# Spare products, late modulation and scan loads moved in a one-core f32 MLA + DeltaNet + ConvGLU layer

## The chip, the cores and the metric

One core of one Trainium2 chip runs the whole layer in one launch. The metric is the device time of one execution in microseconds (us); lower is better. A run of a kernel is timed several times, and a separate execution is recorded by the hardware profiler. PE is the matmul engine (TensorE), DVE the vector engine (VectorE), ACT the scalar engine (ScalarE), POOL is GpSimd, and SP (SyncE) issues most of the DMA transfers. Each engine carries out its own list of instructions in order, and waits where an operand or a buffer isn't ready.

## The reference, cut to what matters

One layer over 256 latent tokens `x` and 256 context tokens `ctx`, width 2048, all in f32. Only the latent stream is put out.

```
sh1,sc1,g1,sh2,sc2,g2 = split(silu(c) @ w_ada + b_ada)        # modulation, 6 x 2048
p      = modulate(rmsnorm(x), sh1, sc1) @ w_in                # columns split into:
         q_a, kv_a, k_r (attention), dq, dk, dv, dz, da, db (DeltaNet), two gates
y_mla  = attention of 8 heads: q from rmsnorm(q_a) @ w_q_b, k and v from
         rmsnorm(kv_a) @ w_kv_b, rms norm over q and k, rotary part, softmax over
         256 latent and 256 context keys
y_dn   = gated DeltaNet of 8 heads in chunks of 64, one scan forward, one backward,
         started from the final states of the context
y      = (sigmoid(gate_mla) * (y_mla @ w_o_mla) + sigmoid(gate_dn) * (y_dn @ w_o_dn)) @ w_out
x      = x + g1 * y
x      = x + g2 * (silu(dwconv(h @ w_gate)) * (h @ w_val)) @ w_down,
         h = modulate(rmsnorm(x), sh2, sc2)
```

## The kernel before, in words

**Products.** Every weight comes in as f32. `load_w` brings it into a ring of eight raw buffers of 128x1024 (tag `raw`), and splits each half of 512 columns: ACT casts the high part `whi` (L122), DVE subtracts it from the raw weight and so makes the low part `wlo` (L123). `split` does the same for activations. `mm_hl` multiplies a tile of 128x128: `whi` with the high and low parts of the activation side by side (128x512), then `wlo` with the high part (128x256). These two are called a pair here. `row_bcast` spreads a column vector over all partitions by f32 products with the identity.

**Stages.** Modulation and first projections (names `amp`, `fp`) to about 141 us of the profiled span; the first heads' projections (`mmp`) with the decay masks of the DeltaNet (`cps`, `gp`, `eps`), to about 195; the other heads' DeltaNet chains, to about 430; the latent attention (`kps`, `vps`, `qps`, `sps`, `yps`), to about 720; the DeltaNet scan over eight steps (`yp`, `kp`, `sp_`, `op`), to about 901; the products of the two branches (`brp`); the output product (`ops`), 948 to 1041; the norm before the FFN; the FFN's up products (`fps`) to 1527, and its down products (`dps`).

**Late modulation.** The part of the modulation that is needed late is 128 tiles of 128x1024 f32 (`rawa`, in the same ring as the weights). `ada_rest` loads two ahead, and one multiply-reduce on DVE (L268 within the scan and the stages behind it, an operation that the order lists as ISA) sums a tile against `sch`, a row that is read back from memory (`Sc`). Column blocks 0 to 2 must be done before the norm of the FFN.

**Order.** `Side` is a generator with a budget: a call adds nanoseconds, and the generator goes on as long as it has budget; a tile of late modulation costs 1300. Budgets: `ADB` in the DeltaNet chains, `AD` in the attention, `ADS` in the scan, `WO` per output tile, 1000 per FFN tile. `fill` is another such generator: it brings the products of gate tiles (`gtp`, 16 pairs each, yielding after each four) between the attention's and the scan's steps. With `pe.pinned` true, PE's products stand in the order in which the code issues them; otherwise, and on the other engines, the compiler's scheduler chooses. SP's DMAs go in the order of issue; in the compiled program each also waits for the landing of the DMA eight before it.

**The scan.** `scan()` allocates its memory at the place that the attention's last products (`yps`) free. For a step it loads V, the triangular system (`tt`, six small loads from `Xq` and `Xo`) and the keys `KEs`, and KTs, all into `jit` and `tt`. The first step has no state yet, so that its KTs aren't used. `warm(n)` issues n spare products with the identity that compute nothing, two records each.

Of the kernel before, what the change touches and what calls it, by code (L numbers as in the profile page):

```python
# [42 lines left out]
OC = 4000  # L43
WO = 1500
IK = 7000
# [3 lines left out]
R1 = 0.9  # L49
ADB = 4000  # L50
SCALE = 192.0 ** -0.5


@with_exitstack
def hybrid_block(ctx: ExitStack, tc: tile.TileContext, io, dbg=None):
# [88 lines left out]
    def lazy_w(src):  # L144

        cur = [None, None]

        def W(o, m=P):
            if cur[0] != o // GR:
                cur[:] = o // GR, load_w(src[:, o // GR * GR : min(o // GR * GR + GR, src.shape[1])])  # L150
            return cur[1](o % GR, m)

        return W

# [32 lines left out]
    class Rms:  # L187
# [17 lines left out]

        def finish(self, mul, out):
            n, pl = self.n, self.pl
            ms = pl.tile([P, 4], F32, tag="ms", name="ms", bufs=1)[:, :n]
            dve.tensor_scalar(out=ms, in0=self.ss[:, :n], scalar1=mul, scalar2=EPS, op0=ALU.mult, op1=ALU.add)
            rsq(pl, ms, ms, n)  # L210
            bc_ps = psa.tile([P, 512], F32, tag="aux", name="bc_ps")
            row_bcast(bc_ps, ms, n)
            if out is not None:
                act.copy(out.rearrange("p a b -> p (a b)"), bc_ps[:, : n * P])
            return bc_ps

    def rms_bcast(pl, K, src, mul, out):
        r = Rms(pl, K, len(src(0)))
        for k in range(K):
            r.add(*src(k))  # L220
        return r.finish(mul, out)

# [236 lines left out]
    mod_cols(0, False, *later)  # L459
    warm(9)  # L460
    H = [hp.tile([P, KD, 2, T], F32R, tag="h", name="h0"), ph.tile([P, KD, 2, T], F32R, tag="h", name="h1")]
# [316 lines left out]
    ada.done, ada.bound = 0, True  # L778
    ins = {h: head_inputs(h) for h in (3, 0)}

# [115 lines left out]

    def gate_tiles(jobs):

        for w, f, out, fin in jobs:
            W = lazy_w(io[w][f])  # L900
            ps = psm.tile([P, 512], F32, tag="mm", name="gtp")
            for k in range(KD):
                mm_hl(ps, P, W(k * P), H[0][:, k], k == 0, k == KD - 1)
                if k == 3 and late:
                    late.pop()()
                if k % 4 == 3 and k < KD - 1:
                    yield 1300
            gate_fin(ps, out, fin)
            yield 1300
# [21 lines left out]
    bq = pn.tile([P, 1, T], F32, name="bq")  # L931
    rms_bcast(pn2, 4, lambda k: (qax[:, k],), 1.0 / 512, bq)
    for k in range(4):
# [31 lines left out]
    fill(5200)  # L965
    bk = rms_bcast(pn2, 4, lambda k: (kvx[:, k, 0], kvx[:, k, 1]), 1.0 / 512, None).rearrange("p (a b) -> p a b", a=2)
    fill(9000)
# [10 lines left out]
    def mm3(ps, a, b, first, last):  # L978

        pe.matmul(ps, a[0], b[0], start=first, stop=False)  # L980
        pe.matmul(ps, a[0], b[1], start=False, stop=False)
        pe.matmul(ps, a[1], b[0], start=False, stop=last)

    def mla_project(b):
# [58 lines left out]
        v_tile(1)  # L1043
        yield 3500
        v_tile(2)
        v_tile(3)
# [4 lines left out]
        k_scale(km0, 0)  # L1051
        for j in range(2):
            q_tile(j)
        k_scale(km1, 1)
        yield 3500
# [124 lines left out]
    fill.finish()  # L1180
    gates = gate_tiles([("wgd", f, f - GD0, None) for f in range(GD0, KD)])
    pC.close()
# [34 lines left out]
    def scan():  # L1217
        pS = ExitStack()
        ps1 = pS.enter_context(pool_("scan", 1, "right"))
        jit = ps1.tile([P, 6, 1024], F32, name="jit")  # L1220
        TTv = [ps1.tile([P, HEADS, 64], F32, name=f"tt{n}") for n in range(2)]
        av = ps1.tile([P, HEADS, 64], F32, name="av")
        for n in range(2):
            pool.memset(TTv[n], 0.0)
        half_ = [slice(0, 64), slice(64, 128)]
        S = ps1.tile([P, HEADS, 2, P], F32, name="S")
        steps = (4, 5, 6, 7, 0, 1, 2, 3)

        def load_kv(n):
            kt, v = (jit[:, 2 * j + n % 2].rearrange("p (h c) -> p h c", c=P) for j in (0, 2))  # L1230
            sync.dma_start(kt, KTs[steps[n]])
            sync.dma_start(v, Vs[steps[n]])
            return kt, v
# [10 lines left out]
        def load_ke(n):  # L1244
            ke = jit[:, 2 + n % 2].rearrange("p (h c) -> p h c", c=P)
            sync.dma_start(ke, KEs[steps[n]])
            return ke
# [10 lines left out]
        for n, st in enumerate(steps):  # L1258
# [23 lines left out]
            if last:  # L1282
                zo = jit[:, 2:4].rearrange("p a (h t) -> p (a h) t", t=T)
                sync.dma_start(zo, Zs)
# [365 lines left out]
```

## Time and profile before

| | |
|---|---|
| time, median of 3 runs | 1770.11 us (1768.79 to 1772.45) |
| the profiled execution | 1771.28 us |
| its span | 1769.5 us |
| PE busy | 1743.7 us, 99% |
| DVE busy | 1324.0 us, 75% |
| ACT busy | 939.4 us, 53% |
| mean granted clock of PE | 0.996 |
| moved by DMA | 415.08 MB, 235 GB/s on the mean |

The profile is one execution recorded by the hardware. A row of a timeline starts with its start in us and the time that it lasts; then engine, line of the kernel, operation, output<-inputs, the shape, how many instructions it holds, and in brackets the idle time of the engine before it with what ended it. A row of a group has the number of instructions, then busy us in all and mean ns of one, then the idle time before them and what ended most of it. In a row of waits stand the us waited in all, how often, and the longest. Windows give busy us of PE, PEld (PE's weight loads), DVE, ACT and POOL in a stretch, the granted clock of PE (1.00 is full speed), the busy share of the DMA engines and GB/s.

### The profile page before, as it was taken

Reading aid. Unit: us, or ns where it says so; the run is one execution under the profiler, and the core shown is the slowest. Engines: PE = TensorE matmul, PEld = TensorE weight load, DVE = VectorE, ACT = ScalarE, POOL = GpSimd, SP = SyncE. Lnnn points to the kernel's source line nnn. Section 1 sums busy time; section 2 is a strip of 40 time slices with the busy share of each in tenths; the row PEclk is TensorE's granted clock in tenths of the full one; section 3 lists DMA queues with packets and bytes.
Section 4 is the critical chain, followed back from the end, with each engine's and each line's share of the span. In section 5 each row is a group of like instructions: output and inputs, shape, how many; then the busy total and the mean of one; then the engine's idle time right before and its main releaser. Section 6 shows DMA issues by size and latency. Waiting matters only on the chain.

```text
span 1769.5 us, 34499 instructions
## 1 busy us (share of the span) xinstructions
PE 1743.7 (99%) x13173; PEld 1517.7 (86%) x13173; DVE 1324.0 (75%) x2576; ACT 939.4 (53%) x1953; POOL 48.6 (3%) x49
## 2 busy tenths in 40 slices
PE   8999999999999999999999999999999999999999
PEld 6788888888888988887888898888888888888888
DVE  4687788769777878586789789888778888755554
ACT  3335544444666666555656455555555555544443
POOL 0000011000000000000010000000000000000000
PEclk9999999999999999999999999999999999999999
DMA  9992588783677867997967858777666777666662
GB/s 382 392 365 93 167 233 245 228 257 117 215 245 249 263 206 261 296 328 244 332 192 239 290 175 288 228 224 236 215 191 225 225 226 226 207 199 199 199 196 86
DMA packets 188710, 415.08 MB, mean 235 GB/s; under 512 B 56768, under 2 KB 95040, under 8 KB 186240
## 3 DMA queue, kind: packets, MB, share of 16 engines
q1 hardware_dynamic: 162944, 397.92, 69.0%
q10 hardware_dynamic: 25600, 14.96, 2.7%
q8 instruction: 103, 1.69, 0.4%
q14 instruction: 63, 0.52, 0.1%
HBM read 386.21 MB, written 26.48 MB: 233 GB/s over the span
## 4 chain that ended last, share of the span: by engine, by line
PE 89%; DMA 6%; DVE 3%; issue 1%; ACT 1%; POOL 0%; SPq 0%; DVEq 0%; ACTq 0%; POOLq 0%
PE fps L69 27%; PE dps L69 14%; PE mmp L69 13%; PE gtp L69 9%; PE ops L69 5%; PE brp L69 4%; PE fp L69 4%; PE vps L69 1%; DMA raw<-in_wadab 1%; PE kps L69 1%; PE amp L69 1%; DVE wlo L123 1%; PE sps L69 1%; PE tp L69 1%; DMA raw<-in_wgd 1%
## 5 line engine op out<-in xcount | busy, mean ns | idle before, releaser
L123 DVE TENSOR_TENSOR wlo<-raw,whi 128x512 fp32r<-128x512 f32 (+1 forms) x940 | 634.9, 685 | 228.9 <-ACT whi L122 218.9
L122 ACT CAST whi<-raw 128x512 fp32r<-128x512 f32 (+1 forms) x940 | 572.9, 619 | 377.6 <-PE dps L69 113.7
L69 PE MATMUL fps<-H,whi 128*128 128x512 f32 x1376 | 472.4, 392 | 0.0
L69 PE MATMUL fps<-H,wlo 128*128 128x256 f32 x1376 | 371.4, 280 | 0.0
L69 PEld LDWEIGHTS fps<-H,whi 128*128 128x128 f32 x1376 | 252.5, 188 | 50.7 <-DVE fx L509 0.2
L69 PEld LDWEIGHTS fps<-H,wlo 128*128 128x128 f32 x1376 | 258.4, 188 | 7.4 <-DVE wlo L123 0.5
L69 PE MATMUL gtp<-h,whi 128*128 128x512 f32 x640 | 230.5, 398 | 0.2
L69 PE MATMUL mmp<-h,whi 128*128 128x512 f32 x640 | 226.8, 397 | 0.0
L69 PE MATMUL dps<-GB,whi 128*128 128x512 f32 (+1 forms) x595 | 195.7, 378 | 0.0
L69 PE MATMUL gtp<-h,wlo 128*128 128x256 f32 x640 | 173.4, 281 | 2.6 <-DVE wlo L123 2.5
L69 PE MATMUL mmp<-h,wlo 128*128 128x256 f32 x640 | 175.8, 281 | 0.0
L69 PE MATMUL dps<-GB,wlo 128*128 128x256 f32 x560 | 154.1, 280 | 0.0
L69 PEld LDWEIGHTS gtp<-h,whi 128*128 128x128 f32 x640 | 119.3, 188 | 25.3 <-ACT whi L122 1.2
L69 PEld LDWEIGHTS mmp<-h,whi 128*128 128x128 f32 x640 | 119.0, 188 | 24.7 <-issue 0.4
L69 PEld LDWEIGHTS gtp<-h,wlo 128*128 128x128 f32 x640 | 120.5, 188 | 8.4 <-DVE wlo L123 4.2
L69 PEld LDWEIGHTS dps<-GB,whi 128*128 128x128 f32 x595 | 109.2, 188 | 21.2
L69 PEld LDWEIGHTS mmp<-h,wlo 128*128 128x128 f32 x640 | 120.3, 188 | 2.7 <-issue 0.6
L268 DVE CUSTOM_DVE_ANT_0 rawa<-rawa,sch 128x1024 f32<-128x1024 f32 x71 | 86.6, 1221 | 29.3 <-DMA rawa<-in_wada 29.1
L69 PEld LDWEIGHTS dps<-GB,wlo 128*128 128x128 f32 x560 | 105.1, 188 | 0.6
L69 PE MATMUL fp<-h,gh 128*128 128x256 f32 (+1 forms) x448 | 84.3, 289 | 0.7 <-DVE h L69 0.7
L69 PEld LDWEIGHTS fp<-h,gh 128*128 128x128 f32 (+1 forms) x448 | 68.8, 188 | 6.1 <-issue 4.5
L69 DVE CUSTOM_DVE_ANT_0 rawa<-rawa,sch 128x1024 f32<-128x1024 f32 x57 | 69.1, 1217 | 0.0
(564 smaller groups left out, 2553.2 us busy)
## 6 DMA issues: line engine op xcount, KB each, us to landing
rawa<-in_wada SPq DMA_DIRECT2D x128, 512.0 KB, 4.6
raw<-in_wgate SPq DMA_DIRECT2D x82, 512.0 KB, 4.4
raw<-in_wval SPq DMA_DIRECT2D x82, 512.0 KB, 5.0
raw<-in_wdown SPq DMA_DIRECT2D x80, 512.0 KB, 4.3
wt<-in_wadas SPq DMA_DIRECT2D x16, 1024.0 KB, 10.2
raw<-in_wadab SPq DMA_DIRECT2D x32, 512.0 KB, 11.9
raw<-in_wgm SPq DMA_DIRECT2D x32, 512.0 KB, 4.6
raw<-in_wgd SPq DMA_DIRECT2D x32, 512.0 KB, 6.2
```

The lines of the kernel that those rows point to most:

```text
L69: i = f(*a, **k)
L122: act.copy(hi, raw)
L123: dve.tensor_tensor(out=lo, in0=raw, in1=hi, op=ALU.subtract)
L268: (odve if ada.bound else dve).tensor_tensor_reduce(out=w, in0=w, in1=sch, scale=1.0, scalar=0.0, op0=ALU.mult, op1=ALU.add, accum_out=par ...
```

## The change

Eight edits:

1. `WO` is 1100 in place of 1500: a smaller budget of late modulation per output tile.
2. `ADE` = 0.35: the projections of the first two heads call late modulation between their products, which they did not.
3. `warm` blocks shrink: 9 to 7 in the modulation, 7 and 7 to 3 and 4, and 14 to 7 at the norm of the FFN.
4. `finish` of the norm calls a side: between the reciprocal root on POOL and the broadcast, four pairs of a gate tile are issued, in both norms of the attention's ranks.
5. `k_scale` (8 calls) broadcasts a vector in another way: DVE spreads it on diagonals (`diag`, a high and a low part), and two f32r products of 128x512 with a matrix of ones replace four f32 products of 128x128. DVE's part is issued one or two `v_tile`s ahead.
6. In the last attention block late modulation is left out from the second step on, not from the fifth on.
7. `gate_tiles` in the scan asks for its weights a portion ahead: `need(1)` at k = 4, the next branch's weights at k = 12, and a branch asks for the next gate tile's first portion at k = 3.
8. The scan's memory is laid out anew, so that what the first step loads (`jit0`, `tt0`) lies in memory that is free before the attention ends. The first step's KTs is not loaded.

```diff
-WO = 1500
+WO = 1100
+ADE = 0.35
...
     def lazy_w(src):
-        cur = [None, None]
+        got = {}
+        def need(i):
+            if i not in got:
+                got[i] = load_w(src[:, i * GR : min(i * GR + GR, src.shape[1])])
         def W(o, m=P):
-            if cur[0] != o // GR:
-                cur[:] = o // GR, load_w(src[:, o // GR * GR : min(o // GR * GR + GR, src.shape[1])])
-            return cur[1](o % GR, m)
+            need(o // GR)
+            return got[o // GR](o % GR, m)
+        W.need = need
         return W
...
             rsq(pl, ms, ms, n)
+            side(1300)
             bc_ps = psa.tile([P, 512], F32, tag="aux", name="bc_ps")
...
-    warm(9)
+    warm(7)
...
-    ins = {h: head_inputs(h) for h in (3, 0)}
+    ins = {h: head_inputs(h, lambda c: ada(c * ADE)) for h in (3, 0)}
...
+            W = Ws[j] if Ws else lazy_w(io[w][f])
             for k in range(KD):
+                if Ws and k == 4:
+                    W.need(1)
+                if Ws and k == 12:
+                    after(j)
...
+    def diag(r):
+        rh = pc2.tile([P, 4], F32R, tag="rb_h", name="rb_h")
+        rl = pc2.tile([P, 4], F32, tag="rb_l", name="rb_l")
+        dve.tensor_copy(rh, r)
+        dve.tensor_tensor(out=rl, in0=r, in1=rh, op=ALU.subtract)
+        idb = ident.unsqueeze(1).broadcast_to([P, 4, P])
+        dg = []
+        for v in (rh, rl):
+            d = pc2.tile([P, 4, P], F32R, tag="rb_d", name="rb_d")
+            dve.tensor_tensor(out=d, in0=idb, in1=v.unsqueeze(2).broadcast_to([P, 4, P]), op=ALU.mult)
+            dg.append(d)
+        return dg
...
         def k_scale(km, h2):
+            dg = diag(km)
+            yield 500
             bp = psa.tile([P, 512], F32, tag="aux", name="kbp")
-            row_bcast(bp, km, 4)
+            for n in range(2):
+                pe.matmul(bp, onesr, dg[n].rearrange("p a b -> p (a b)"), start=n == 0, stop=n == 1)
...
-                    side(c, R1 if b < 3 else 2.0, b == 3 and n > 3)
+                    side(c, R1 if b < 3 else 2.0, b == 3 and n > 0)
...
+    bW, gW = {}, [lazy_w(io["wgd"][f]) for f in range(GD0, KD)]
+    gates = gate_tiles([("wgd", f, f - GD0, None) for f in range(GD0, KD)], gW, branch_next)
...
-        W = load_w(io[w][f])
+        W = load_w(io[w][f]) if wh else bW.pop(f)
...
             if k == 3:
                 yield 1300
+                if not wh:
+                    gate_next(f + 1)
...
-        jit = ps1.tile([P, 6, 1024], F32, name="jit")
-        TTv = [ps1.tile([P, HEADS, 64], F32, name=f"tt{n}") for n in range(2)]
+        jit = ps1.tile([P, 4, 1024], F32, name="jit")
+        TTv = [None, ps1.tile([P, HEADS, 64], F32, name="tt1")]
...
+        jit0 = ps1.tile([P, 2, 1024], F32, name="jit0")
+        TTv[0] = ps1.tile([P, HEADS, 64], F32, name="tt0")
...
-            sync.dma_start(kt, KTs[steps[n]])
+            if n:
+                sync.dma_start(kt, KTs[steps[n]])
             sync.dma_start(v, Vs[steps[n]])
...
-        warm(7)
+        warm(3 + rms.k - 1)
...
-    warm(14)
+    warm(7)
```

Where instructions moved, at three places. First SP's list around the first loads of the scan; `raw` are weights, `rawa` late modulation, `jit` and `tt` the scan's operands. Before:

```order
L249 DMA rawa<-in_wada 128x1024
L128 DMA raw<-in_womla 128x1024
L128 DMA raw<-in_wgd 128x1024 x2
L128 DMA raw<-in_womla 128x1024
L249 DMA rawa<-in_wada 128x1024 x2
L128 DMA raw<-in_wgd 128x1024
L249 DMA rawa<-in_wada 128x1024
L1231 DMA jit<-KTs 128x1024
L1232 DMA jit<-Vs 128x1024
L1241 DMA tt_8700<-Xq 32x8x32 x2
L1241 DMA tt_8700<-Xo 32x8x32
```

and of the changed kernel, at the same place of SP's list:

```order
L129 DMA raw<-in_womla 128x1024
L255 DMA rawa<-in_wada 128x1024
L129 DMA raw<-in_wgd 128x1024 x2
L255 DMA rawa<-in_wada 128x1024
L129 DMA raw<-in_womla 128x1024
L1284 DMA jit_8778<-Vs 128x1024
L1293 DMA tt_8779<-Xq 32x8x32 x2
L1293 DMA tt_8779<-Xo 32x8x32
L1293 DMA tt_8779<-Xq 32x8x32 x2
L1293 DMA tt_8779<-Xo 32x8x32
L1298 DMA jit_8778<-KEs 128x1024
```

The load of KTs is gone, and weights of the second branch product stand ahead of V and the system in the place of late modulation.

Second, DVE's list in the first heads, where the decay gate `gx` is worked out (`plx` is a polynomial of it, `ghl` its high and low parts, `B` the masks built from it). Before:

```order
L570 TENSOR_SCALAR plx<-w2x 128x64
L123 TENSOR_TENSOR wlo<-raw,whi 128x512
L572 SCALAR_TENSOR_TENSOR plx<-plx,w2x 128x64 x6
L573 SCALAR_TENSOR_TENSOR plx<-plx,zx 128x64
L575 SCALAR_TENSOR_TENSOR xg<-plx,xg 128x64
L579 SCALAR_TENSOR_TENSOR gx<-xg,ea 128x64
```

and of the changed kernel:

```order
L578 SCALAR_TENSOR_TENSOR plx<-plx,w2x 128x64
L70 ISA rawa,parts<-rawa,sch 128x1024
L70 ISA parts 128x1
L578 SCALAR_TENSOR_TENSOR plx<-plx,w2x 128x64
L124 TENSOR_TENSOR wlo<-raw,whi 128x512
L578 SCALAR_TENSOR_TENSOR plx<-plx,w2x 128x64 x2
L579 SCALAR_TENSOR_TENSOR plx<-plx,zx 128x64
L124 TENSOR_TENSOR wlo<-raw,whi 128x512
L581 SCALAR_TENSOR_TENSOR xg<-plx,xg 128x64
L585 SCALAR_TENSOR_TENSOR gx<-xg,ea 128x64
```

The first three rows stand there three times one after the other, and a fourth tile of late modulation stands some rows above; before, none of the 128 stood ahead of `gx`.

Third, DVE's list in a step of the scan (`r` is the new value's right side, `gk` a finished gate, `ox` and `t` the branch product's end). Before:

```order
L509 TENSOR_TENSOR gk<-gtp,gk 128x256
L268 ISA rawa,parts<-rawa,sch 128x1024
L268 ISA parts 128x1
L1210 SCALAR_TENSOR_TENSOR ox<-brp,ox 128x256
L1211 SCALAR_TENSOR_TENSOR t_8685<-gt,ox 128x256
L1276 SCALAR_TENSOR_TENSOR r<-kp,negc,jit 128x128 x8
L123 TENSOR_TENSOR wlo<-raw,whi 128x512 x4
```

and of the changed kernel, around the eight `r` of such a step:

```order
L515 TENSOR_TENSOR gk<-gtp,gk 128x256
L124 TENSOR_TENSOR wlo<-raw,whi 128x512
L274 ISA rawa,parts<-rawa,sch 128x1024
L274 ISA parts 128x1
L1256 SCALAR_TENSOR_TENSOR ox<-brp,ox 128x256
L1257 SCALAR_TENSOR_TENSOR t_8754<-gt,ox 128x256
L1328 SCALAR_TENSOR_TENSOR r<-kp,negc,jit_8778 128x128 x8
L124 TENSOR_TENSOR wlo<-raw,whi 128x512 x2
```

Before, four low parts stood behind the eight `r`; in the changed kernel two stand behind it, and the others ahead of it.

More of the change, by code (lines that the diff above doesn't have):

```diff
@@ L204, in add_sq, with finish @@
             self.k += 1
-        def finish(self, mul, out):
+        def finish(self, mul, out, side=lambda c: None):
             n, pl = self.n, self.pl
@@ L215, in finish, with rms_bcast @@
             return bc_ps
-    def rms_bcast(pl, K, src, mul, out):
+    def rms_bcast(pl, K, src, mul, out, side):
         r = Rms(pl, K, len(src(0)))
@@ L220, in rms_bcast @@
             r.add(*src(k))
-        return r.finish(mul, out)
+        return r.finish(mul, out, side)
     class Side:
@@ L895, in gate_fin, with gate_tiles @@
                 late.pop()()
-    def gate_tiles(jobs):
-        for w, f, out, fin in jobs:
-            W = lazy_w(io[w][f])
+    def gate_tiles(jobs, Ws=None, after=None):
+        for j, (w, f, out, fin) in enumerate(jobs):
+            W = Ws[j] if Ws else lazy_w(io[w][f])
             ps = psm.tile([P, 512], F32, tag="mm", name="gtp")
             for k in range(KD):
+                if Ws and k == 4:
+                    W.need(1)
+                if Ws and k == 12:
+                    after(j)
                 mm_hl(ps, P, W(k * P), H[0][:, k], k == 0, k == KD - 1)
@@ L931, in hybrid_block @@
     bq = pn.tile([P, 1, T], F32, name="bq")
-    rms_bcast(pn2, 4, lambda k: (qax[:, k],), 1.0 / 512, bq)
+    rms_bcast(pn2, 4, lambda k: (qax[:, k],), 1.0 / 512, bq, fill)
     for k in range(4):
@@ L965, in hybrid_block @@
     fill(5200)
-    bk = rms_bcast(pn2, 4, lambda k: (kvx[:, k, 0], kvx[:, k, 1]), 1.0 / 512, None).rearrange("p (a b) -> p a b", a=2)
+    bk = rms_bcast(pn2, 4, lambda k: (kvx[:, k, 0], kvx[:, k, 1]), 1.0 / 512, None, fill).rearrange("p (a b) -> p a b", a=2)
     fill(9000)
@@ L1044, in mla_project @@
         yield 3500
+        sc0, sc1 = k_scale(km0, 0), k_scale(km1, 1)
+        next(sc0)
         v_tile(2)
+        next(sc1)
         v_tile(3)
@@ L1050, in mla_project @@
         qsq = pc2.tile([P, 3, T], F32, tag="qsq", name="qsq", bufs=1)
-        k_scale(km0, 0)
+        for _ in sc0:
+            pass
         for j in range(2):
             q_tile(j)
-        k_scale(km1, 1)
+        for _ in sc1:
+            pass
         yield 3500
@@ L1180, in hybrid_block, with branch_next, gate_next @@
     fill.finish()
-    gates = gate_tiles([("wgd", f, f - GD0, None) for f in range(GD0, KD)])
+    bW, gW = {}, [lazy_w(io["wgd"][f]) for f in range(GD0, KD)]
+    def branch_next(f):
+        if f < KD:
+            bW[f] = load_w(io["womla"][f])
+    def gate_next(f):
+        if f < len(gW):
+            gW[f].need(0)
+        else:
+            branch_next(f)
+    gates = gate_tiles([("wgd", f, f - GD0, None) for f in range(GD0, KD)], gW, branch_next)
     pC.close()
@@ L1219, in scan @@
         ps1 = pS.enter_context(pool_("scan", 1, "right"))
-        jit = ps1.tile([P, 6, 1024], F32, name="jit")
-        TTv = [ps1.tile([P, HEADS, 64], F32, name=f"tt{n}") for n in range(2)]
+        jit = ps1.tile([P, 4, 1024], F32, name="jit")
+        TTv = [None, ps1.tile([P, HEADS, 64], F32, name="tt1")]
         av = ps1.tile([P, HEADS, 64], F32, name="av")
+        half_ = [slice(0, 64), slice(64, 128)]
+        S = ps1.tile([P, HEADS, 2, P], F32, name="S")
+        for tag, shape, bufs in (("r", [P, 4, P], 2), ("y", [P, 2, 4, P], 1), ("qe", [P, HEADS, P], 1), ("osq", [P, 4, 2, 64], 2)):
+            for _ in range(bufs):
+                ps1.tile(shape, F32, tag=tag, name=tag, bufs=bufs)
+        jit0 = ps1.tile([P, 2, 1024], F32, name="jit0")
+        TTv[0] = ps1.tile([P, HEADS, 64], F32, name="tt0")
         for n in range(2):
             pool.memset(TTv[n], 0.0)
-        half_ = [slice(0, 64), slice(64, 128)]
-        S = ps1.tile([P, HEADS, 2, P], F32, name="S")
         steps = (4, 5, 6, 7, 0, 1, 2, 3)
         def load_kv(n):
-            kt, v = (jit[:, 2 * j + n % 2].rearrange("p (h c) -> p h c", c=P) for j in (0, 2))
-            sync.dma_start(kt, KTs[steps[n]])
+            kt, v = (x.rearrange("p (h c) -> p h c", c=P) for x in ((jit[:, 2], jit[:, 3]) if n % 2 else (jit[:, 0], jit0[:, 0])))
+            if n:
+                sync.dma_start(kt, KTs[steps[n]])
             sync.dma_start(v, Vs[steps[n]])
@@ L1244, in load_ke @@
         def load_ke(n):
-            ke = jit[:, 2 + n % 2].rearrange("p (h c) -> p h c", c=P)
+            ke = (jit[:, 1] if n % 2 else jit0[:, 1]).rearrange("p (h c) -> p h c", c=P)
             sync.dma_start(ke, KEs[steps[n]])
@@ L1282, in scan @@
             if last:
-                zo = jit[:, 2:4].rearrange("p a (h t) -> p (a h) t", t=T)
+                zo = jit[:, 0:2].rearrange("p a (h t) -> p (a h) t", t=T)
                 sync.dma_start(zo, Zs)
```

## The prediction

> **What bounds the kernel now.** I read the head of the page first (busy shares, then the chain that ended last).
>
> ```profile
> span 1769.5 us, 34499 instructions
> PE 1743.7 (99%) x13173; PEld 1517.7 (86%) x13173; DVE 1324.0 (75%) x2576; ACT 939.4 (53%) x1953; POOL 48.6 (3%) x49
> PE 89%; DMA 6%; DVE 3%; issue 1%; ACT 1%; POOL 0%; SPq 0%; DVEq 0%; ACTq 0%; POOLq 0%
> ```
>
> PE is busy for 1743.7 of 1769.5 us, so PE's products are the time: the kernel gets shorter only where products disappear, where one of PE's 26 us of gaps closes, or where PE runs at a higher granted clock. Work added on DVE or DMA is free as long as PE does not wait for it. So I took each edit to its place on PE's timeline and asked which wait, or which product, goes there. The profiled execution took 1771.28 us (1.78 around the span) against the median of 1770.11; the sum is made against 1771.28.
>
> **A. Spare products at the seam before the FFN.** The timeline of PE, ACT, DVE and POOL there, and PE's group of spares (two records for a spare):
>
> ```profile
> L69 PE MATMUL warm<-ident 128*128 128x128 f32 x80 | 10.2, 280 | 0.0
> 1041.47 1.83 PE L69 MATMUL warm<-ident 128*128 128x128 f32 x14
> 1041.86 0.42 ACT L1456 ACTIVATE x1q<-x 128x256 f32<-128x256 f32 x1
> 1043.23 0.31 PE L69 MATMUL ss<-ones,x1q 128*32 128x1 f32 x16
> 1043.47 1.83 PE L69 MATMUL warm<-ident 128*128 128x128 f32 x14
> 1043.84 0.70 POOL L174 TENSOR_TENSOR ms<-ms,half 128x2 f32<-128x2 f32 x1 [145.11 <-DVE ms L1471]
> 1045.13 0.61 PE L69 MATMUL b<-ident,ms 128*128 128x128 f32 x4
> 1045.58 3.29 PE L69 MATMUL warm<-ident 128*128 128x128 f32 x28
> 1046.84 0.88 DVE L1485 SCALAR_TENSOR_TENSOR H<-h,adaT,H 128x256 fp32r<-128x256 f32 x2 [0.19 <-ACT H L1484]
> ```
>
> One spare takes 3.29 / 14 = 0.235 us (10.2 / 40 = 0.26 over all). First block, 7 to 3: its operand x1q is ready at 1041.86 + 0.42 = 1042.28, the product started at 1043.23; three spares end at about 1042.25, so 0.95 us go. Second, 7 to 4: POOL's ms ends 1044.54, the product b started 1045.13; POOL's work hangs on the sum in front of it and moves along with it, and four spares cover all but 0.1 of it, so 0.5 go. Third, 14 to 7: 7 x 0.235 = 1.6, they would end at 1047.2, and the FFN's first low part H on DVE (two tiles in the row) is done at 1046.84 + 0.44 = 1047.28, so PE would hardly wait; but the other tiles of H come in DVE's pace, and I let 0.7 of the 1.6 be lost to it. The two spares taken from the modulation stage stand before a wait of PE anyway and give 0. **A: -2.3** (0 to -3.4).
>
> **B. Row broadcast of the k norm** (8 calls): four f32 products of 128 columns become two f32r products of 512.
>
> ```profile
> L69 PE MATMUL kbp<-ident,km 128*128 128x128 f32 x64 | 8.6, 277 | 0.0
> L69 PE MATMUL sps<-kt,qt 128*128 128x512 f32 x48 | 14.6, 413 | 0.0
> L69 PE MATMUL gp<-B,onesr 64*128 64x512 f32 x16 | 4.2, 468 | 0.0
> L123 DVE TENSOR_TENSOR wlo<-raw,whi 128x512 fp32r<-128x512 f32 (+1 forms) x940 | 634.9, 685 | 228.9 <-ACT whi L122 218.9
> 560.00:580.00 20.00, 20.00 (x178) 17.52 (x177) 13.41 (x30) 12.90 (x31) 3.29 (x2) 1.00 0.71 212
> ```
>
> Before, a call costs 8.6 / 8 = 1.07 us of PE. The same two products are not in the trace; the neighbours are 128x512 products of the attention, 14.6 / 48 = 0.30, and of the masks against onesr, 4.2 / 16 = 0.26. Two of them: 0.52 to 0.61, so 8 calls save 3.7 to 4.4. I take -4.1. DVE gets per call two multiplies of 128x512 (0.69 each by wlo) and two tiny ones, about 1.7 us, 14 us in all. What hides it: DVE is busy 13.41 of 20 us in the MLA stage (the window above; its columns after the length are PE, PEld, DVE and ACT), and the multiplies are issued one or two v tiles ahead of the products. Where a weight's low part queues behind them, PE waits; two-sided, 0 to +2, I take +1. **B: -3.1** (-4.4 to -1.7).
>
> **C. Gate products during the reciprocal root.** PE's group for the broadcast of a rank norm:
>
> ```profile
> L69 PE MATMUL bc_ps<-ident,ms 128*128 128x128 f32 x20 | 3.0, 290 | 2.0 <-POOL ms L174 2.0
> ```
>
> PE idles 2.0 us in front of these for POOL. Of its calls two get four pairs of a gate tile (eight such products ahead of each), 1.4 us or more of work that was due anyway, which covers 0.9 each. **C: -1.5** (0 if that tile's low weight parts come late, -2.0 at most).
>
> **D. First step of the scan.** Timelines of PE, SP and DVE, and the windows of 20 us (last columns: granted clock, DMA share, GB/s):
>
> ```profile
> 704.61 1.23 DVE L268 CUSTOM_DVE_ANT_0 rawa<-rawa,sch 128x1024 f32<-128x1024 f32 x1 [1.23 <-DMA rawa<-in_wada]
> 706.83 1.67 PE L69 MATMUL yps<-PT,V 128*128 128x512 f32 x8 [1.64 <-DVE PT L123]
> 716.23 0.30 SPq L1241 DMA_DIRECT2D tt<-Xo  x1
> 719.19 2.52 PE L69 MATMUL yp<-jit,tt 64*64 64x128 f32 x32 [2.36 <-DMA tt<-Xo]
> 722.23 0.41 PE L69 MATMUL brp<-YM,wlo 128*128 128x256 f32 x1
> 722.87 0.41 PE L69 MATMUL brp<-YM,wlo 128*128 128x256 f32 x1
> 700.00:720.00 20.00, 16.00 (x95) 13.47 (x97) 14.84 (x28) 10.75 (x24) 0.53 (x1) 0.98 0.66 190
> 720.00:740.00 20.00, 20.00 (x163) 17.17 (x159) 6.32 (x16) 10.51 (x27) 0.00 (x0) 0.85 0.99 302
> ```
>
> The window of 700 to 720 holds PE's largest gap: 4 of 20 us. Two waits make it. yps waited 1.64 because DVE's PT stood behind a late-modulation tile that itself waited for its DMA; the change takes late modulation out of that block, so some 1.4 go. Then yp waited 2.36 for the last tt load, issued only at 716.23, eight DMAs after the load of jit (which had to wait for memory of the attention). With step 0 loading into memory that is free already, the queue has no such wait at its head: the tt loads can all be issued some 5 us earlier, and 2.36 goes. Third, after that gap the clock is down: 0.85 over 720 to 740 is (1 - 0.85) x 20 = 3.0 us lost, and a pair of products takes 722.87 - 722.23 = 0.64 there. No gap, no drop: 3.2. The gate products brought forward by C (2.8 us for two calls) are missing here, so PE arrives at yp 2.8 us and the vanished waits earlier; that is why I do not call it safe. **D: -7.0** (-1.4, if only the first wait goes, to -8.0).
>
> The trace has the lower clock right behind an idle time of 2.36 us, and none behind the idle times of 1.64 here or 1.55 and 1.82 below. The Trainium skill (TensorE: Matmul & The Clock Gate, section "What's actually happening") has the half rate come only after an idle window of about 3.4 us. By that figure alone the drop would not belong to this gap, the clock would not return with it, and the sum would end 3.2 us higher; here the trace disagrees with it, and the trace decides.
>
> **E. Gate weights of the scan a portion ahead.** Waits of the engines between 686 and 902 us, and the longest of these on DVE and PE:
>
> ```profile
> PEld gtp L69 <- DVE wlo L123: 4.2, 5, 1.9
> PE gtp L69 <- DVE wlo L123: 2.5, 4, 1.6
> PEld gtp L69 <- ACT whi L122: 1.2, 4, 0.5
> 801.78 2.16 DVE L1276 SCALAR_TENSOR_TENSOR r<-kp,negc,jit 128x128 f32<-128x128 f32 x8 [2.52 <-PE kp L69]
> 803.86 2.48 DVE L123 TENSOR_TENSOR wlo<-raw,whi 128x512 fp32r<-128x512 f32 x4
> 804.60 0.39 PE L69 MATMUL gtp<-h,wlo 128*128 128x256 f32 x1 [1.55 <-DVE wlo L123]
> ```
>
> A low part asked for only when its product is due queues behind the scan's r on DVE (2.52 of wait and 2.16 of work), and PE stops. A portion ahead, two low parts stand before r in DVE's order. I take 3.0 of the 4.2 + 1.2. **E: -3.0** (0 to -5.4).
>
> **F. Fewer late-modulation tiles in the output product.** DVE there, and PE's group:
>
> ```profile
> L69 PE MATMUL ops<-MB,wlo 128*128 128x256 f32 x128 | 33.8, 283 | 2.8 <-DVE wlo L123 2.8
> 1001.15 1.23 DVE L268 CUSTOM_DVE_ANT_0 rawa<-rawa,sch 128x1024 f32<-128x1024 f32 x1 [2.69 <-DMA rawa<-in_wada]
> 1003.38 0.39 PE L69 MATMUL ops<-MB,wlo 128*128 128x256 f32 x1 [1.82 <-DVE wlo L123]
> ```
>
> All 2.8 us stand behind a tile that waits for its DMA in DVE's queue. Ten of them stand between the first and the last output tile in place of fourteen: **F: -1.8** (0 to -2.8).
>
> **G. What it costs: the first heads.**
>
> ```profile
> L268 DVE CUSTOM_DVE_ANT_0 rawa<-rawa,sch 128x1024 f32<-128x1024 f32 x71 | 86.6, 1221 | 29.3 <-DMA rawa<-in_wada 29.1
> 149.52 1.52 DVE L572 SCALAR_TENSOR_TENSOR plx<-plx,w2x 128x64 f32<-128x64 f32 x6
> 151.60 0.22 DVE L579 SCALAR_TENSOR_TENSOR gx<-xg,ea 128x64 f32<-128x64 f32 x1
> 151.92 1.08 PE L69 MATMUL cps<-gx,masks 128*128 128x64 f32 x8 [0.23 <-issue]
> 140.00:160.00 20.00, 19.77 (x110) 14.37 (x108) 15.71 (x43) 9.99 (x23) 0.00 (x0) 1.00 0.24 84
> ```
>
> Nine tiles of 1.22 us enter DVE's order here. Four of them and a further low part or two stand ahead of gx, which moves from 151.6 to about 157. PE's order has 24 more products, twelve pairs of 0.35, ahead of cps, so PE is there at about 156; but the last of those pairs need low parts that stand behind the three tiles between the plx steps (at about 155.3 on DVE, where PE would be at 153.8). I take 1.6 us of new idle for the 0.23 of now. **G: +1.4** (0 to +5).
>
> **Sum.** -2.3 - 3.1 - 1.5 - 7.0 - 3.0 - 1.8 + 1.4 = -17.3; from 1771.28: **1754 us**, 0.9% under the median.
>
> **The rivals.**
>
> *The waits only move* (few of D to F is gained). For it: E and F are waits for DVE, and DVE gets 14 us more, is in order, and 29.1 us of its tiles' waits for DMA remain; PE comes to yp earlier than now. Against: SP's list has no blocked load ahead of tt any more. A + B + C in full and 1.4 of D, less G: -2.3 - 3.1 - 1.5 - 1.4 + 1.4 = -6.9, **1764 us**.
>
> *The first heads turn the sign.* The place is 141 to 200 us; the mechanism, each late-modulation tile on DVE stands between a mask and the product that needs it, and three waits of PE above some 2.4 us each bring the clock down as at 720. Price: nine tiles x 1.3 = 11.7 and three drops x 3.2 = 9.6, so 21.3 in place of 1.4: 1754 + 20 = **1774 us**. It decides once PE's idle time there passes about 2.3 us at a time. Against it: DVE is busy only 15.71 of 20 us at the start of the stage, and PE got twelve more pairs to stand on.
>
> *The spares held the clock.* With 16 of 40 spares gone, PE could idle at the seam and run the FFN's first 6.4 us at half clock: the 3.2 us of D come back there and A is nothing, 1754 + 2.3 + 3.2 = **1760 us**. Against it: no idle time worked out under A is above 1 us, and 1.82 us at 1003 left the clock up. The Trainium skill (same page, section "Why this matters for your kernels") forbids PE gaps above about 3 us, and none of that length arises here.
>
> **How the numbers follow.** My forecast, 1748 to 1759: 0.58. The waits only move, 1759 to 1768: 0.24. The seam's clock: 0.08. The first heads, up to 1776: 0.10. 0.2% of the median, 3.5 us, is about what a measurement of this kernel can tell from no change. Faster by more than that (below 1766.6) hold the forecast, the seam and most of the first rival: 0.83. Within it: 0.10. Slower: 0.07. The range from 1746 (all of E, F and C) to 1766 leaves 2 in 10 out.
>
> **What would show it.** A: rows of spares at the seam of 6, 8 and 14, and no idle time in front of ss and b above 0.3 us. B: kbp as 16 products of 0.26 to 0.30. C: no wait of bc_ps for POOL. D: granted clock of 1.00 through the first 40 us of the scan, and no wait of yp for a DMA. E and F: the waits of gtp and ops for wlo under 1.5 us in the stage. G: PE idle for 1 to 2 us shortly before cps. The forecast is wrong if the clock is down anywhere between 141 and 200, if yp still waits for tt, or if PE shows new waits for wlo between 430 and 690, where DVE took on the diagonals.

## The result, and the profile after

The changed kernel takes 1759.03 us in the median of 6 runs (1757.88 to 1759.98), against 1769.45 us of before in 6 runs. The ratio is 0.9946, with a 95% interval of 0.9932 to 0.9959: 0.54% faster, where 0.9% was forecast. The profiled execution took 1757.95 us. The head of its page, those of its waits of PE that bear on the change (us in all, times, longest), and its windows around the first step of the scan:

```profile
span 1756.1 us, 34353 instructions
PE 1733.0 (99%) x13093; PEld 1507.0 (86%) x13093; DVE 1333.7 (76%) x2608; ACT 943.1 (54%) x1953; POOL 48.5 (3%) x49
```

```profile
PE bc_ps L70 <- POOL ms L179: 1.6, 3, 0.8
PE fps L70 <- DVE H L1537: 1.4, 1, 1.4
PE yps L70 <- DVE PT L124: 1.1, 1, 1.1
PE vps L70 <- DVE mns L1126: 1.0, 1, 1.0
PE ops L70 <- DVE wlo L124: 1.0, 1, 1.0
PE gtp L70 <- ACT whi L123: 1.0, 1, 1.0
PE yp L70 <- DMA tt<-Xo: 0.9, 1, 0.9
PE sps L70 <- DVE qt L1099: 0.7, 1, 0.7
PE gtp L70 <- DVE wlo L124: 0.5, 1, 0.5
```

```profile
700.00:720.00 20.00, 17.85 (x127) 15.07 (x126) 13.49 (x25) 11.20 (x25) 0.00 (x0) 1.00 0.81 265
720.00:740.00 20.00, 20.00 (x182) 17.15 (x181) 11.50 (x25) 14.83 (x37) 0.00 (x0) 1.00 0.92 286
```

PE's busy time fell by 10.7 us. Of the waits named in the prediction, those of gtp and ops for wlo are nearly gone (2.5 to 0.5, 2.8 to 1.0), that of yp is less than half, that of bc_ps is hardly smaller (2.0 to 1.6), and four are new: vps and sps wait for DVE in the attention, fps for H in the FFN, and gtp in the scan for a high part from ACT. The granted clock is full behind yp, where it was 0.85. Ahead of the last yps stand on DVE:

```profile
704.63 1.22 DVE L274 CUSTOM_DVE_ANT_0 rawa<-rawa,sch 128x1024 f32<-128x1024 f32 x1
705.78 1.89 DVE L124 TENSOR_TENSOR wlo<-raw,whi 128x512 fp32r<-128x512 f32 x3
707.59 0.68 DVE L124 TENSOR_TENSOR PT<-ptp,PT 128x512 fp32r<-128x512 f32 x1
```

A tile of late modulation is still there, and three low parts, so PT is no earlier (707.59; before, it started at 706.09).

One profile against another would have told this as -13.4 us of span. The runs say less, because the times of before scatter by more than 10 us from execution to execution (1760.98 to 1773.36 in 31 runs on one chip), together with the mean granted clock that is listed with each run. So I compare two things: the runs with their mean clock, and stages of the profiles, each the difference of two start times of PE's products. Each ratio is against the runs of before that were made beside it.

```
kernel        runs  median us  ratio to before, 95%        mean clock
before          31    1768.83  1                           0.9974
after            6    1759.03  0.9946  [0.9932, 0.9959]    0.9987
b_scanmem       10    1768.07  1.0005  [0.9990, 1.0021]    0.9974
b_gates         10    1766.00  0.9996  [0.9981, 1.0011]    0.9966
b_spares_yp     10    1766.90  0.9996  [0.9981, 1.0010]    0.9979
b_kscale        10    1771.83  1.0024  [1.0009, 1.0040]    0.9949
b_wo_ade        10    1771.48  1.0017  [1.0000, 1.0035]    0.9965
a_oldkscale     10    1765.32  0.9990  [0.9975, 1.0005]    0.9976
a_oldspares     10    1759.48  0.9950  [0.9936, 0.9965]    0.9983
a_pinfill       10    1769.04  1.0007  [0.9991, 1.0022]    0.9951
a_nofill        12    1764.83  0.9981  [0.9969, 0.9993]    0.9962
a_hold_act      12    1762.63  0.9974  [0.9959, 0.9989]    0.9960
a_pooldiag       6    1760.02  0.9955  [0.9940, 0.9970]    0.9985
a_ffnhold        6    1758.54  0.9947  [0.9929, 0.9965]    0.9983
```

Names with b_ are the kernel before with something added, names with a_ the changed kernel with something altered. The row of before holds one of its four sets (31, 31, 23 and 11 runs; medians 1766.54 to 1768.83, mean clocks 0.9973 to 0.9980). Against these medians the changed kernel's 1759.03 us is 7.5 to 9.8 us less, so the 10.4 us against the six runs beside it are at the upper end. A mean clock lower by 0.001 is about 0.001 x 1765 = 1.8 us, an estimate that takes the time as PE's.

```
us from       qk      kps     yps     yps     sp_    ops     ss     fps
to            kps     yps     last    sp_     brpYD  ss      fps    dps
before       68.61   93.16  165.54   18.46  177.27  92.87   7.39  478.39
b_scanmem    71.77   93.00  165.69   13.06  178.88  94.04   7.39  478.42
b_gates      68.60   93.13  166.09   13.80  173.78  94.78   7.39  478.41
b_spares_yp  71.53   93.03  165.81   14.66  176.13  95.47   7.39  478.40
b_kscale     71.76   91.42  169.96   13.34  177.15  93.01   7.39  478.42
b_wo_ade     71.49   93.08  167.14   13.32  174.49  94.47   7.39  482.28
after        71.71   91.01  165.53   11.39  172.49  90.61   4.81  480.22
a_oldkscale  71.70   92.69  169.09   11.55  172.47  91.53   4.81  480.21
a_oldspares  71.69   90.98  164.89   11.02  173.95  91.18   7.39  478.39
a_pinfill    81.80   91.00  167.63   10.87  172.44  92.70   4.82  480.21
a_nofill     71.47   91.78  169.31   14.15  172.46  89.82   4.81  480.22
a_hold_act   73.29   90.99  165.38   16.87  172.02  91.45   4.82  478.65
a_ffnhold    71.73   91.01  165.94   10.60  173.96  90.84   4.81  478.61
```

qk is the last product of the DeltaNet chains, "last" the last yps, sp_ the scan's first sp, brpYD the first product of the second branch; from brpYD to ops it is 44.53 us in every profile. The table's first surprise is its first row: the 18.46 us from the last yps to the scan's first sp, on which term D of the prediction stands, were 13.3 to 13.8 in three other profiles whose edits leave the scan's loads as before (b_gates, b_kscale, b_wo_ade), with the same 48 gate products in this stretch.

### The profile page after: what moved, and what is told of

The parts are those of the page before. It is cut to its first block, busy times and chain, and to the rows that moved or that the text cites. A ratio compares the mean times of both kernels' runs of the same rounds, so it can differ in the third digit from the quotient of the medians.

```text
span 1756.1 us, 34353 instructions
## 1 busy us (share of the span) xinstructions
PE 1733.0 (99%) x13093; PEld 1507.0 (86%) x13093; DVE 1333.7 (76%) x2608; ACT 943.1 (54%) x1953; POOL 48.5 (3%) x49
## 4 chain that ended last, share of the span: by engine, by line
PE 89%; DMA 5%; DVE 3%; issue 1%; ACT 1%; SPq 0%; POOL 0%; POOLq 0%; ACTq 0%; DVEq 0%
PE fps L70 27%; PE dps L70 14%; PE mmp L70 13%; PE gtp L70 10%; PE brp L70 5%; PE ops L70 4%; PE fp L70 4%; DMA raw<-in_wadab 1%; PE vps L70 1%; PE amp L70 1%; PE kps L70 1%; DVE wlo L124 1%; PE tp L70 1%; DMA rawa<-in_wada 1%; PE kp L70 1%
## 5 line engine op out<-in xcount | busy, mean ns | idle before, releaser
L274 DVE CUSTOM_DVE_ANT_0 rawa<-rawa,sch 128x1024 f32<-128x1024 f32 x64 | 78.1, 1222 | 32.4 <-DMA rawa<-in_wada 32.3
```

Source lines behind the costliest of these rows:

```text
L274: (odve if ada.bound else dve).tensor_tensor_reduce(out=w, in0=w, in1=sch, scale=1.0, scalar=0.0, op0=ALU.mult, op1=ALU.add, accum_out=par ...
```

## The experiments

**Single edits on the kernel before.**

```diff
 b_scanmem: edit 8 alone
-        jit = ps1.tile([P, 6, 1024], F32, name="jit")
+        jit = ps1.tile([P, 4, 1024], F32, name="jit")
...
+        jit0 = ps1.tile([P, 2, 1024], F32, name="jit0")
+        TTv[0] = ps1.tile([P, HEADS, 64], F32, name="tt0")
 b_gates: edit 7 alone
+                if Ws and k == 4:
+                    W.need(1)
...
 b_spares_yp: nine spares in the wait
+            if first:
+                warm(9)
             for h in range(HEADS):
                 for d in range(2):
                     pe.matmul(yp[d][half_[d ^ h % 2], h // 2], tt[half_[d], h], rs[h // 4][half_[d], h % 4], start=True, stop=True)
 b_kscale: edit 5 alone
...
-            row_bcast(bp, km, 4)
+            for n in range(2):
+                pe.matmul(bp, onesr, dg[n].rearrange("p a b -> p (a b)"), start=n == 0, stop=n == 1)
...
```

> Kernel before with edit 8 alone (the scan's memory; the first step's KTs not loaded). Theory: the queue was held by memory, so the last load of the system is issued some 4 us earlier, yp waits 0.5 us or less for it, the granted clock stays at 1.00 behind it, and the scan's first sp comes 5 to 6 us earlier than before, all of it kept to the end (about -5 us, near 1764). The wait of yps (1.6 us) stays, since that is not a wait for memory. Rival: the landing of the loads in a full DMA sets it, not their issue; then yp waits 1 to 2 us, the clock depends on which, and the gain is 1 us without the clock or 4 us with it.

> Kernel before with edit 7 alone (gate weights of the scan a portion ahead). Theory: waits of the gate products for whi and wlo in the scan go on their own account: between the first sp and the last product of the scan 3 to 5 us less, the wait of yp and the lower clock behind it as before (0 there). Rival: in the changed kernel the 4.8 us of that stretch came from what edit 8 or the smaller number of tiles did to the order; then less than 1.5 us go here.

> Kernel before with nine spare products (2.1 us of work that computes nothing) ahead of the first yp, where PE idled for 2.4 us. Theory: the idle time is what brought the clock down; yp starts when it did (within 0.3 us), the clock stays at 1.00 behind it, and everything from the first sp on comes 3 us earlier (near -3 us of time). Rival: the idle time is not the cause, the clock is 0.85 in the 20 us behind it as before, and the time is the same or up to 1 us longer.

> Kernel before with edit 5 alone (the k norm's row broadcast over diagonals). Theory of the prediction, mended by the profile after: PE has 3.0 us less of kbp, DVE 14 us more; from the first vps to the last yps the stretch is 3 us shorter and no new wait over 0.5 us shows (near -3 us). Rival: DVE's extra work comes back as waits of vps, sps or kbp behind it, as in the changed kernel (1.2, 0.9 and 0.4 us there), and the stretch is 1 to 2 us shorter.

None is faster alone, and b_kscale is slower (by 0.24%; its interval, 1.0009 to 1.0040, leaves out 1). SP's timeline of b_scanmem, then PE's of b_kscale, then PE's of b_spares_yp:

```profile
711.16 1.63 SPq L1247 DMA_DIRECT2D tt<-Xq  x2
715.20 0.30 SPq L1247 DMA_DIRECT2D tt<-Xo  x1
```

```profile
578.34 0.39 PE L69 MATMUL vps<-whi,kvn 128*128 128x256 f32 x1 [2.21 <-ACT uo L872]
661.43 1.10 PE L69 MATMUL kbp<-rb_d,onesr 128*128 128x512 f32 x2 [0.85 <-DVE rb_d L994]
709.87 2.79 PE L69 MATMUL yps<-PT,V 128*128 128x512 f32 x8 [2.21 <-DVE PT L123]
721.36 1.10 PE L69 MATMUL yp<-jit,tt 64*64 64x128 f32 x32
```

```profile
719.64 2.17 PE L69 MATMUL warm<-ident 128*128 128x128 f32 x18
721.74 1.10 PE L69 MATMUL yp<-jit,tt 64*64 64x128 f32 x32
```

With the memory laid out anew, the last system load is still issued at 715.20, one us earlier than in the profile of before. What SP waited for ahead of that load stands in its rows of waits, of before and then of b_scanmem:

```profile
SPq L1241 <- DMA jit<-KTs: 1.6, 1, 1.6
SPq L1247 <- DMA rawa<-in_wada: 2.4, 1, 2.4
```

In both it is the landing of an earlier transfer. No wait for memory shows in either: in the profile of before KTs is issued at 707.88, 0.43 us after the tile of late modulation ahead of it, and the first system load at 709.03. Nor did the moment of issue decide. The load of V in before and then in b_scanmem (last column: us from issue to landing):

```profile
jit<-Vs SPq DMA_DIRECT2D x1, 512.0 KB, 10.2
jit<-Vs SPq DMA_DIRECT2D x1, 512.0 KB, 8.0
```

V landed at 718.5 us in before and at 717.0 in b_scanmem. In before the first system load, issued at 709.03, landed at 718.6, and the last, issued 7.2 us later, at 719.6; in b_scanmem the last landed at 718.0. The six small loads land right behind V, so what edit 8 gains there is likely the 512 KB of KTs, no longer loaded ahead of V. The first theory fell; its rival (the landing sets it) holds for the loads, though yp does not wait in this profile and the time is that of before.

In b_kscale, where the loads are as before, yp does not wait either: PE came to it at 721.36, after the loads had landed (720.6), where it had come at 716.83 in before (719.19 less the wait). So the wait of 2.36 us is a race between PE and the loads, which other kernels with the same loads run differently. Whether it is in every execution of before is not shown, since one was profiled. In b_spares_yp the spares fill the wait, and the clock is 1.00 behind them. The time does not change: the interval is -3.4 to +1.8 us, so the 3 us expected are just inside it.

b_gates shows its gain where it was expected (177.27 to 173.78), and not in the time: its other stretches got longer (yps waits 2.5 us, ops 3.5) and its clock is lower. b_kscale saves 1.7 us up to the first yps and then loses 4.4 to waits and clock (0.91 in the window from 700). In its runs the mean clock is 0.0031 under that of the before beside it (0.9980), by the estimate above 5.5 us, which is all of its loss.

**Edits undone or varied in the changed kernel, and edits 1 and 2 alone.**

```diff
 b_wo_ade: before with edits 1 and 2
-WO = 1500
+WO = 1100
+ADE = 0.35
...
 a_oldkscale: edit 5 undone
...
+            row_bcast(bp, km, 4)
...
 a_oldspares: edit 3 undone
...
-    warm(7)
+    warm(14)
 a_pinfill: order kept around both norms of edit 4
+    pe.pinned = True
     rms_bcast(pn2, 4, lambda k: (qax[:, k],), 1.0 / 512, bq, fill)
+    pe.pinned = False
...
 a_nofill: edit 4 undone
-    rms_bcast(pn2, 4, lambda k: (qax[:, k],), 1.0 / 512, bq, fill)
+    rms_bcast(pn2, 4, lambda k: (qax[:, k],), 1.0 / 512, bq, lambda c: None)
...
```

> Kernel before with edits 1 and 2 (WO 1100 and late modulation in the first heads). Theory: these two are one edit; the nine tiles done in the first heads leave 10 in place of 14 between the first and the last output tile, the waits of ops for wlo (2 to 3.5 us in the profiles of before and of the single edits, with the clock lowered behind them in four of five) shrink to about 1 us, and the first heads cost under 1 us: 3 to 5 us less. Rival: they carry little, the first heads give back what the output product gains (within 1.5 us of before).

> The changed kernel with edit 5 undone. Theory: edit 5 costs time, since its 3 us of PE come back as waits of vps, kbp and sps for DVE, and each such wait can lower the clock; undone, the attention has no wait of vps or kbp over 0.5 us, and the time is 2 to 5 us under the changed kernel's, a ratio to before of about 0.992. Rival: the other edits leave DVE enough room, and undoing it costs 2 to 3 us of PE (ratio about 0.997).

> The changed kernel with edit 3 undone (all the spares of before). Theory: 2.6 us of the seam come back up to the first fps, but the wait of fps for H (1.5 us, some 18 us later) goes, since PE is later and DVE isn't; 1 to 1.5 us longer than the changed kernel. Rival of the spares as a hold on the clock: the time is the same or less, with a higher mean clock.

> The changed kernel with PE's order kept as written around both rank norms, so that the eight gate products of edit 4 stand right ahead of the broadcast (in the changed kernel the scheduler put them further ahead, and bc_ps waits 0.6 and 1.0 us as before). Theory: both waits fall under 0.3 us, 1.2 to 1.6 us less up to the first kps, and the lower clock seen in these windows (380 to 400 and 440 to 460) does not come: 1 to 3 us less than the changed kernel. Rival: the gate products wait for their own weights there, and nothing is gained.

> The changed kernel with edit 4 undone (no gate products in the rank norms). From the profiles so far the waits of bc_ps are the same with and without it, so it should gain nothing by itself. Theory 1: it is neutral; the first gate tiles only move, kps comes 2.8 us earlier, yp 2.8 us later, and time and mean clock are the changed kernel's. Theory 2: it is worth about 2 us as cover of the clock, which was lowered between 380 and 460 us in four of six profiles of kernels without it and in none of three with it; then the windows there show 0.91 here, the mean clock falls by 0.001 and the time rises by 2 us.

**b_wo_ade** is the theory's miss: the first heads cost little, but the output product is no shorter (94.47) and the FFN is longer. Waits of PE and DVE in it between 930 and 1045:

```profile
PE ops L70 <- DVE wlo L124: 4.1, 4, 2.2
DVE rawa L269 <- DMA rawa<-in_wada: 19.8, 11, 3.7
```

and DVE's of before:

```profile
DVE rawa L268 <- DMA rawa<-in_wada: 14.1, 12, 2.7
```

Ten tiles stand between the first and the last output tile as in the changed kernel, and late modulation waits longer for its DMA than with fourteen. It is not the count alone that shortens this stage in the changed kernel. What else does is not settled; no edit in between was tried together with these two.

**a_oldkscale** refutes the theory that b_kscale had suggested. Edit 5 undone costs 0.44% here. Its wait of vps, and DVE's rows at the same place in the changed kernel:

```profile
579.20 0.36 PE L70 MATMUL vps<-whi,kvn 128*128 128x256 f32 x1 [2.11 <-DVE mns L1104]
```

```profile
577.38 0.68 DVE L1126 CUSTOM_DVE_ANT_0 s__7081<-kbc,sps 128x512 f32<-128x512 f32 x1
577.99 1.22 DVE L70 CUSTOM_DVE_ANT_0 rawa<-rawa,sch 128x1024 f32<-128x1024 f32 x1
579.14 0.21 DVE L1128 TENSOR_SCALAR mns<-mns,qm 128x1 f32<-128x1 f32 x1
```

The wait of vps is there without edit 5. In DVE's order, with edit 5 and without it, a tile of late modulation stands between two short steps of the softmax, which then takes 1.22 us longer. So this wait comes from where the tiles lie, which nearly every edit shifts.

**a_oldspares** is the same in time as the changed kernel: the seam (the norm ahead of the FFN) gets 2.6 us longer, the FFN 1.8 shorter, and the clock does not differ. DVE and PE of the changed kernel in the FFN's first tiles:

```profile
1048.62 1.22 DVE L274 CUSTOM_DVE_ANT_0 rawa<-rawa,sch 128x1024 f32<-128x1024 f32 x1
1051.27 0.87 DVE L1537 SCALAR_TENSOR_TENSOR H<-h,adaT,H 128x256 fp32r<-128x256 f32 x2
```

```profile
1051.90 0.48 PE L70 MATMUL fps<-H,whi 128*128 128x512 f32 x1 [1.37 <-DVE H L1537]
```

PE comes earlier, DVE does not: a tile of late modulation and low parts stand ahead of H.

**a_pinfill** takes the waits of bc_ps away (0.3 us is left), and loses the whole gain. Its rows of PE and its windows:

```profile
389.44 1.08 PE L70 MATMUL rp<-krf,rope 64*64 64x256 f32 x2 [3.23 <-DMA rope<-in_rope]
406.86 0.50 PE L70 MATMUL mmp<-h,whi 128*128 128x512 f32 x1 [2.63 <-DVE kvx L515]
```

```profile
380.00:400.00 20.00, 15.57 (x166) 12.63 (x161) 9.90 (x30) 6.08 (x15) 0.70 (x1) 0.74 0.66 203
400.00:420.00 20.00, 17.37 (x90) 14.77 (x89) 16.81 (x34) 6.77 (x15) 0.00 (x0) 0.91 0.31 97
```

The pinned sums and broadcasts came ahead of the projections that had covered the load of the rotary table and DVE's work, so PE stood for 3.23 and 2.63 us and the clock went to 0.74. The stretch to kps took 10 us more.

**a_nofill** shows what edit 4 is worth, though the waits of bc_ps are nearly the same with and without it (1.6 and 2.0 us). Windows and broadcast of a_nofill, then the same of the changed kernel:

```profile
420.00:440.00 20.00, 19.11 (x223) 15.99 (x222) 17.72 (x36) 9.29 (x22) 2.11 (x3) 0.96 0.48 146
440.00:460.00 20.00, 19.96 (x96) 16.77 (x94) 16.14 (x32) 10.91 (x21) 0.00 (x0) 0.87 0.63 189
438.86 2.07 PE L70 MATMUL bc_ps<-ident,ms 128*128 128x128 f32 x8 [0.89 <-POOL ms L179]
```

```profile
440.00:460.00 20.00, 19.15 (x135) 16.25 (x136) 15.15 (x33) 11.31 (x22) 1.07 (x1) 1.00 0.69 217
443.02 1.16 PE L70 MATMUL bc_ps<-ident,ms 128*128 128x128 f32 x8 [0.85 <-POOL ms L179]
```

Theory 2 holds in size: undone, edit 4 costs 0.35%, and the intervals do not overlap. a_pooldiag, run beside a_nofill with edit 4 in place, took 1760.02 us against its 1764.83. The mean clock falls by 0.0025, by the estimate above 4 of the 6 us. That the place is this stage is likely from the profiles, not shown: the clock was lowered between 380 and 460 in five of seven profiles without edit 4, and in one of six with it in its own order. Why it is lowered behind one wait of 0.89 us and not behind another of 0.85 stays open; a_nofill also lost clock at 700 (0.91), where its yps waited 4.6 us for DVE in place of 1.1, so a part of the 6 us may be late modulation's place again.

**Variants meant to be faster.**

```diff
 a_ffnhold, and first half of a_hold_act
-        ada(1000)
+        if f > 3:
+            ada(1000)
 a_hold_act, second half
+            st, tt, q = steps[n], TTv[n % 2], sync if n else act
...
+                    q.dma_start(tt[rs, :, cs], x[n : n + 2].rearrange("a g c i -> c (a g) i"))
 a_pooldiag
-            dve.tensor_tensor(out=d, in0=idb, in1=v.unsqueeze(2).broadcast_to([P, 4, P]), op=ALU.mult)
+            pool.tensor_tensor(out=d, in0=idb, in1=v.unsqueeze(2).broadcast_to([P, 4, P]), op=ALU.mult)
```

> The changed kernel with two edits at separate places: late modulation is held off in the first four FFN tiles (it is caught up behind them), and the first step's system is loaded by ACT's queue in place of SP's. Theory: the late-modulation tile in DVE's order ahead of H makes the wait of fps (1.5 us) and the longer FFN; from the first fps to the first dps 478.4 us as before in place of 480.2. With the loads out of SP's queue yp does not wait (0.7 to 1.1 us now). Together 2 to 2.5 us under the changed kernel. Rivals: DVE is full there by low parts alone, so the FFN stays at 480; and the loads land no earlier from another queue, since the DMA engines are full.

> The changed kernel with the two wide multiplies of edit 5 on POOL in place of DVE (POOL is busy 3%). Theory: DVE's 11 us less between 460 and 700 take away the waits of vps and sps (1.2 and 0.9), 1 to 2 us under the changed kernel. Rival: those waits are made by late modulation in DVE's order and stay, or POOL is so slow that kbp waits for it; then the same or up to 4 us longer.

> The changed kernel with late modulation held off in the first four FFN tiles, without the loads on ACT's queue. Theory: from the first fps to the first dps 478.4 to 478.7 us in place of 480.2, nothing else differs; 1.6 us under the changed kernel, near a ratio to before of 0.993 to 0.994. Rival: the tiles come back as waits later in the FFN or in the scan's order, and the ratio is 0.995 as that of the changed kernel or above.

The hold in the FFN does what was expected there, twice: 478.65 and 478.61 in place of 480.22, and no wait of fps. In a_ffnhold the whole is 1758.54 us, 0.5 under the changed kernel and within the noise of both, so no version here is shown to beat it. The loads on ACT's queue went the other way:

```profile
719.14 0.66 PE L70 MATMUL yp<-jit,tt 64*64 64x128 f32 x2 [3.33 <-DMA tt<-Xo]
720.89 1.98 PE L70 MATMUL yp<-jit,tt 64*64 64x128 f32 x30 [1.09 <-DMA tt<-Xo]
720.00:740.00 20.00, 19.11 (x163) 16.49 (x164) 11.24 (x23) 13.58 (x33) 0.00 (x0) 0.88 0.88 272
```

yp waits 4.4 us in all, and here the clock is down behind it. On POOL the multiplies take 1.29 and 1.15 us each, no wait goes, and the time is the changed kernel's, which fits a_oldkscale: those waits are made by where late modulation lies.

## Why the prediction was right, and where it was not

The direction and the range (1746 to 1766) held; the gain was 10.4 us where 17.3 were summed (16.1 against the median of 1770.11 us that was known then). The 1759.03 us lie on the border between the forecast's band (1748 to 1759) and that of "the waits only move". That the total came so near was in part luck: the largest term brought nothing, and edit 4 brought, through the clock, several us that the sum did not hold. By its own steps:

- **What bounds the kernel**: right. PE is busy 99% in both, and taking 11 us off DVE (a_pooldiag) changed nothing.
- **D, -7.0: the step that failed**, and the largest term. It took a wait of 2.36 us and the clock behind it from one execution, and held them for steady. Other profiles with the same loads need 13.3 to 13.8 us for the stretch; the changed kernel needs 11.39, and the 2.8 us of gate products that edit 4 moved out of it (32 stand there in place of 48) make that 14.2. So against these nothing was gained from the last yps to the first sp. The cause was misread too: no wait for memory shows ahead of the scan's loads, the last of them was held by the landing of KTs, and all six landed behind V whenever they were issued. yp still waits for tt (0.9 us), which the prediction had named as a sign of being wrong. And the wait of yps did not go, it is 1.1 in place of 1.6, since the tile ahead of PT bears the line of the late modulation called in the scan (L268 before, L274 after), which the scheduler moves up into the attention; the tiles that edit 6 can take out bear the helper's line (L69). The row quoted in the prediction had said so.
- **C, -1.5**: wrong in the mechanism, right in that it counts. bc_ps still waits, 1.6 of 2.0 us: PE's order is not kept in that stage, and the scheduler put the eight products elsewhere (in the first norm at 381.5, before the sums). What edit 4 is worth, 6 us by undoing it, is mostly clock by the estimate.
- **B, -3.1**: right in kind. The products cost 5.6 us in place of 8.6 (by their group in the profiles), and the stretch from kps to the first yps, with four of the eight calls, is 1.7 us shorter by the edit (b_kscale against before, a_oldkscale against the changed kernel). Alone on before the edit made the kernel 0.24% slower, and undone in the changed kernel it costs 0.44% (6 us, of which the products explain 3.4, twice the 1.7, and 0.0011 of mean clock about 2 by the estimate above). That its worth depends on where late modulation lies is likely, not shown.
- **E, -3.0**: right in direction and size, and in the mechanism in part. The stretch went from 177.27 to 172.49 in the profiles, and 3.5 us by itself in b_gates; kernels without edit 7 have 174.49 to 178.88 there, those with it 172.02 to 173.96. The waits of gtp that PE itself had give only 1.0 us of it: 2.5 us for low parts became 0.5, and 1.0 for a high part is new. Where the rest went is open.
- **F, -1.8**: the prediction gives no working for the 1.8; ten tiles in place of fourteen would take 0.8 off 2.8. The stage is 2.3 us shorter against the profile of before, up to 5 against the other profiles of kernels without the edits. By the count of tiles alone it does not follow (b_wo_ade), and the four single edits on before (93.01 to 95.47) had a granted clock of 0.91 or 0.92 between 1000 and 1020.
- **A, -2.3**: mis-sized. The seam gave 2.6, the FFN took back 1.8 and not 0.7, so 0.75 is left in the profiles and nothing that the runs can tell in the time.
- **G, +1.4**: the first heads cost 0.8 (from the first mmp to the first sp 53.12 to 53.89 us). PE's predicted idle of 1.6 us did not come: cps waits 0.2 us as before, and gx came at 155.5 where about 157 was expected.
- **Rivals**: the first heads did not turn the sign, and the spares did not hold the clock (a_oldspares). "The waits only move" comes nearest: for D it happened, for E and F it did not.

## What to carry to other kernels

Before a wait of a profile becomes a term of a sum, see whether it is in a second execution: where the granted clock moves from run to run, one trace's low clock may be chance and not a price. Before a late issue of a load is called the cause of a wait, look at what the load lands behind. An edit that only shifts work on an engine that is not the bound can be worth nothing alone and something in company, so undo it in the final kernel before judging it. Where a scheduler sets the order, a filler stands where the compiled order has it, not where the code issues it, and pinning it can pin what stood well.

## What the runs showed of the hardware

The granted clock fell after idle times far shorter than I had taken as the limit (2.4 us): to 0.96 and 0.87 over two windows in a_nofill with one idle time of 0.89 us and a run of small sums ahead of it, and not in the changed kernel with 0.85. The same code had it both ways: between 440 and 460 us it was 1.00 in before and b_gates, and 0.91 in b_scanmem, b_spares_yp and b_kscale, whose edits lie behind this place, each with one wait of bc_ps of 0.89 or 0.90 us. The broadcast in before, and the same in b_spares_yp, where it took nearly twice as long:

```profile
440.77 1.16 PE L69 MATMUL bc_ps<-ident,ms 128*128 128x128 f32 x8 [0.90 <-POOL ms L174]
442.22 2.08 PE L69 MATMUL bc_ps<-ident,ms 128*128 128x128 f32 x8 [0.90 <-POOL ms L174]
```

In the 31 runs of the table's before the mean clock lay between 0.994 and 1.000, which goes with a good part of their scatter. The Trainium skill (TensorE: Matmul & The Clock Gate, section "What's actually happening") describes a window of activity that runs freely and is not tied to the kernel's start, so that the point at which the clock changes depends on where in the window the first product lands, and (section "A second HAM failure mode: psum-queue depth-cycling"), for another kernel in bf16, short idle times between groups of products that let the clock oscillate. The traces agree with both, as far as they show the same code with a drop (0.91) and without one (1.00); with a limit of 3.4 us on one idle time, the figure that the prediction cites, they don't, since the longest wait there is 0.90 us.
